# Fifteen seven-product pairs instead of fourteen in each half of the down projection

## The chip, the cores and the metric

The kernel runs on one core of a Trainium2 chip. The metric is the device time of one execution in microseconds (us). Five engines matter here: TensorE (PE: matmuls, with its weight loads PEld), VectorE (DVE), ScalarE (ACT), GpSimd (POOL) and SyncE (SP); the last two mostly issue DMAs in this kernel.

## The reference

One layer of an encoder on 256 positions of width 2048, all in float32: a mixer block (a gated MLP branch and a neighbourhood-attention branch, merged and projected), then a channel mixer, then a final RMSNorm. The change lies in the last matrix product of the channel mixer:

```python
def conv_ffn(x, g_norm, w_up, conv_k, conv_b, w_down):
    h = rms_norm(x, g_norm)
    up = h @ w_up                       # 256 x 2048 by 2048 x 11008
    ...                                 # centred depthwise convolution, width 3
    gate, val = jnp.split(up, 2, axis=-1)
    return x + (jax.nn.silu(gate) * val) @ w_down   # 256 x 5504 by 5504 x 2048
```

## The kernel before

**Precision.** TensorE has to give float32 products, so each operand is split into a high and a low part, and each product is three matmuls: high by high, low by high, high by low (`triple`). For a weight tile that comes from DRAM (`wraw`), ACT makes the high part (`whi`, line 172) and DVE the low part (`wlo`, line 173).

**The down projection.** It is worked off in two halves of 1024 output columns each (`g_dn[0]`, then `g_dn[1]`). The 5504 rows of the weights are 43 chunks of 128 rows: 21 pairs of chunks and a single one. A half therefore has 21 slots, 0 to 20, of two pieces each, and one last piece. A piece is 128 rows by 1024 columns of the weights, 512 KB, loaded by SP into one of five `wraw` buffers.

**Plain and seven-product slots.** A pair of chunks, two blocks of positions and two blocks of columns make a product of 2x2 by 2x2 blocks. A plain slot (P) does it in eight block products: 24 matmuls of 128x512. A seven-product slot does it in seven, by sums of blocks (Strassen's scheme in Winograd's form): 21 matmuls, 9 issued with the first piece (`r == 0`) and 12 with the second (`r == 1`). The sums of the activations are made in the up projection, one set for each pair in `DOWN_PAIRS` (`sums`, `sums_split`), written to DRAM, and read back by POOL's DMA queue (`stored`, line 1416). The sums of the weights come in one of two ways:

- Made slots (M): DVE makes four sums of 128x512 from the raw pieces (`weight_sums`, lines 362 to 366, into the tiles `t13` and `t24`), and ACT and DVE split them into `h13`, `l13`, `h24`, `l24` (`weight_sums_split`, lines 376 and 377), which the 12 matmuls of the second piece read. There is one tile of each name.
- Kept slots (K, the pairs in `DOWN_SPLIT`): the sums were made and split beside the up projection and written to DRAM; POOL's queue reads the four tiles of 512 KB back (`split_read`, line 1270), again into one tile of each name. SP loads only half of such a slot's first piece (256 KB).

**What sets the order.** The code is written out by hand: `begin(i)` issues the load of piece i + 5, the split of piece i + 3 and the tasks noted for piece i; then the matmuls of piece i are issued. A made slot that begins at piece i notes its sums at i - 3 and the split of its sums at i - 2 (`wide`). Reads of the kept sums are noted six pieces ahead, on one in-order queue with the reads of the activations' sums, which have three tiles in turn. Such a read can be issued once the matmuls that read the tile's former content are through. The last of them for `h24` and `l24` is the ninth matmul of a slot's second piece.

In the tiles' names of the profile and of the rows below, `h0` to `h5` are `t13`, `t24`, `h13`, `h24`, `l13`, `l24` of the made slots, and `h6`, `h7` and `s2` the three tiles for the activations' sums.

Of the kernel before, what the change touches and what calls it, by code (L numbers as in the profile page):

```python
# [67 lines left out]
TURN_X2 = (13, 1)  # L68
Y_GAP = 224
PAD = 16  # L70
DOWN_PAIRS = (2, 3, 5, 6, 7, 9, 10, 11, 13, 14, 15, 16, 17, 18)
DOWN_QUADS = ((1, 3, 5, 6, 7, 9, 10, 11, 13, 14, 15, 17, 18, 19), (1, 2, 4, 5, 6, 8, 9, 10, 12, 13, 14, 16, 17, 18))
DOWN_SPLIT = (2, 6, 10, 14, 17)
DOWN_JOBS = ((0, 2), (4, 6), (8, 10), (12, 14), (16, 18))
DOWN_LEADS = ({2: (4, 16, 16), 3: (5,), 5: (8,), 6: (7, 8, 8)}, {})
TWICE_AT = -15
# [4 lines left out]
def trunk_kernel(ctx, tc, x, x_t, vecs, w_in, ln_g, ln_b, w_st, b_s, rpb, w_branch, w_out, w_up, w_down,  # L81
# [26 lines left out]
    def bank():  # L108
        return psum.tile([128, 512], F32, name="bank")
# [76 lines left out]
            split_t[i] = (h, l)  # L186

    tasks = {}
    preload = {}

    def at(i, f):
        tasks.setdefault(i, []).append(f)
# [92 lines left out]

    def wide(src, row0, order, c0, acts, quads, room, done, sums=None, stored=None, split=None, late=False, lead=4, behind=(), ahead={}):
        n0 = plan_wide(src, row0, order, c0)
        boxes = {}
        for q in quads:
            i = n0 + 2 * q  # L290
            k = order[2 * q]
            units[i], units[i + 1] = 1, 2
            b = boxes[q] = {}
            ready = split[0].get(k // 2) if split else None
            if stored:
                b["acts"] = {}
                at(i - (ready[0] if ready else ahead.get(k // 2, lead)), lambda b=b, k=k: stored(k // 2, b["acts"]))
            else:
                b["acts"] = sums[k]
            if ready:  # L300
                halved.add(i)
                for n, lead in zip(("13", "24"), ready[-2:]):
                    at(i - lead, lambda b=b, k=k, n=n: split[1](k // 2, b, n))
                continue
            whole[i] = whole[i + 1] = None
            halves = late and q == quads[0]
            at(i - 3, lambda i=i, b=b, halves=halves: weight_sums(i, b, room, halves))
            if halves:
                at(i - 2, lambda b=b: b.pop("rest")())
            at(i - (1 if q in behind else 2), lambda b=b: weight_sums_split(b, room))  # L310
        return ("wide", n0, order, acts, quads, boxes, done)

# [59 lines left out]
    def weight_sums_split(box, room):  # L372
        u = []
        for name, t in zip(("13", "24"), box.pop("w")):
            h, l = room("h" + name, F32R), room("l" + name, F32R)
            nc.scalar.activation(h, t, AF.Copy)  # L376
            nc.vector.tensor_sub(l, t, h.bitcast(F32))
            u.append((h, l))
        split_sums(box, u)
# [5 lines left out]
    def run_wide(g, tail=0):  # L385
        kind, n0, order, acts, quads, boxes, done = g
# [19 lines left out]
        for i in range(n0, n1 - tail):  # L406
            begin(i)
            q, r = divmod(i - n0, 2)
            if C is None and q in quads:
                c = [bank() for _ in range(8)]  # L410
                P, C = [c[0], c[3], c[5], c[4]], [c[1:3], c[6:]]
            elif C is None:
                c = [bank() for _ in range(4)]
                C = [c[:2], c[2:]]
            if q not in quads:
                for t, c in ((0, 0), (0, 1), (1, 0), (1, 1)) if i > 1 else ((0, 0), (1, 0), (0, 1), (1, 1)):
                    plain(i, t, c)
                split_t.pop(i)
                continue
            st, sp = q == quads[0], q == quads[-1]  # L420
            k, k1 = order[2 * q:2 * q + 2]
            if r == 0:
                if P is None:
                    P = [bank() for _ in range(4)]
                (h0, l0), (h1, l1) = split_t[i], split_t[i + 1]
                triple(P[0], x_of(k, 0), h0[:, 0], l0[:, 0], st, sp)
                triple(C[0][0], x_of(k1, 0), h1[:, 0], l1[:, 0], first(0, 0), False)
                triple(C[0][1], boxes[q]["acts"]["s"][3], h1[:, 1], l1[:, 1], first(0, 1), False)
                split_t.pop(i)
                split_t.pop(i + 1)  # L430
                continue
            S, W = boxes[q]["acts"]["s"], boxes[q]["t"]
            triple(P[1], S[1], *W[1], st, sp)
            triple(P[3], S[0], *W[3], st, sp)
            triple(P[2], S[2], *W[2], st, sp)
            triple(C[1][0], x_of(k1, 1), *W[4], first(1, 0), False)
            if sp:
                done[0](P, i)
        if not tail:
            done[1](C, n1)  # L440
            return
# [803 lines left out]
    for n, (q, i, j) in enumerate(X_SUMS):  # L1245
        sum_acts_at(i, j, first_sums[2 * q], lambda q=q: q,
                    lambda name, dt, i=i: first_room("s2" if name == "f" and i < 16 else name, dt), f"s{n}", True)
# [97 lines left out]
    for n, (pair, g) in enumerate((pair, g) for g in range(2) for pair in OUT_SPLIT[g]):  # L1345
        t_kept[pair, g] = split_rows("out", pair, g)
        i = g_at[2 * n][1]
# [46 lines left out]
    for n, q in enumerate(OUT_PAIRS):  # L1394
        i = g_m2[0][1] + OUT_SUMS[n]
# [29 lines left out]
    def down_order(g):  # L1425
        free = [p for p in range(NF // 2) if p not in DOWN_PAIRS]
        kept = list(DOWN_PAIRS)
# [8 lines left out]
    for p, turn in zip(DOWN_SPLIT, DOWN_JOBS):  # L1436
        for g in range(2):
            d_kept[p, g] = split_rows("down", p, g)
            i = g_up[turn[g]][1]
# [180 lines left out]
```

## Time and profile before

| | |
|---|---|
| median of 3 runs | 1287.13 us (1286.27 to 1287.78) |
| profiled execution | 1286.73 us, of which the span of the instructions 1285.0 us |
| PE busy | 1275.3 us, 99% of the span, 6711 matmuls |
| DVE busy | 1128.1 us, 88% |
| ACT busy | 795.7 us, 62% |
| POOL busy | 173.6 us, 14% |
| DMA | 375.54 MB, mean 292 GB/s |
| granted TensorE clock | 0.999 of full speed |

The busy time of PE counts each matmul until its modelled end, and the ends of pipelined matmuls overlap; what a matmul costs a row of others is the distance from one start to the next. The up projection fills the span from about 604 to 1061 us, the first half of the down projection 1061 to 1169 us, the second 1169 to 1277 us.

### The profile page before, as it was taken

Reading aid. Unit: us, or ns where it says so; the run is one execution under the profiler, and the core shown is the slowest. Engines: PE = TensorE matmul, PEld = TensorE weight load, DVE = VectorE, ACT = ScalarE, POOL = GpSimd, SP = SyncE. Lnnn points to the kernel's source line nnn. Section 1 sums busy time; section 2 is a strip of 40 time slices with the busy share of each in tenths; the row PEclk is TensorE's granted clock in tenths of the full one; section 3 lists DMA queues with packets and bytes.
Section 4 is the critical chain, followed back from the end, with each engine's and each line's share of the span. In section 5 each row is a group of like instructions: output and inputs, shape, how many; then the busy total and the mean of one; then the engine's idle time right before and its main releaser. Section 6 shows DMA issues by size and latency. Waiting matters only on the chain.

```text
span 1285.0 us, 19793 instructions
## 1 busy us (share of the span) xinstructions
PE 1275.3 (99%) x6711; PEld 1088.0 (85%) x6711; DVE 1128.1 (88%) x1675; ACT 795.7 (62%) x1198; POOL 173.6 (14%) x328
## 2 busy tenths in 40 slices
PE   9999999999999999999999999999999999999997
PEld 7888888888888888888888888888888888888885
DVE  7898977777799988997989999899999989989988
ACT  7776575775755555565756666566566656555554
POOL 0003752330000001100000010011001001211210
PEclk9999999999999999999999999999999999999999
DMA  9789879989789977965877888888788779999993
GB/s 368 276 273 285 292 259 346 333 287 324 253 312 366 341 248 253 395 215 180 278 239 259 297 278 251 280 286 272 249 295 294 249 254 343 353 387 333 373 385 129
DMA packets 200485, 375.54 MB, mean 292 GB/s; under 512 B 16320, under 2 KB 124480, under 8 KB 200384
## 3 DMA queue, kind: packets, MB, share of 16 engines
q1 hardware_dynamic: 175472, 285.84, 64.3%
q0 software_dynamic: 24480, 87.78, 19.4%
q8 instruction: 52, 0.85, 0.3%
q10 hardware_dynamic: 432, 0.66, 0.1%
q14 instruction: 49, 0.40, 0.1%
HBM read 323.63 MB, written 48.50 MB: 290 GB/s over the span
## 4 chain that ended last, share of the span: by engine, by line
PE 98%; DVE 1%; issue 0%; ACT 0%; DVEq 0%; ACTq 0%
PE bank L224 31%; PE bank L228 16%; PE bank L321 12%; PE bank L319 11%; PE bank L320 11%; PE bank L252 5%; PE bank L254 5%; PE bank L253 5%; DVE wlo L173 1%; PE bank L873 0%; PE bank L827 0%; PE bank L500 0%; PE bank L862 0%; PE bank L700 0%; PE bank L1052 0%; PE bank L977 0%
## 5 line engine op out<-in xcount | busy, mean ns | idle before, releaser
L173 DVE TENSOR_TENSOR wlo<-wraw,whi 128x1024 fp32r<-128x1024 f32 (+1 forms) x472 | 535.7, 1149 | 113.3 <-ACT whi L172 72.1
L172 ACT ACTIVATE whi<-wraw 128x1024 fp32r<-128x1024 f32 (+1 forms) x472 | 461.1, 993 | 218.6 <-PE bank L320 54.6
L224 PE MATMUL bank<-h,whi 128*128 128x512 f32 x1760 | 423.4, 392 | 0.0
L224 PEld LDWEIGHTS bank<-h,whi 128*128 128x128 f32 x1760 | 323.0, 188 | 61.8
L228 PEld LDWEIGHTS bank<-h,wlo 128*128 128x128 f32 x1760 | 225.9, 191 | 8.8
L228 PE MATMUL bank<-h,wlo 128*128 128x256 f32 x1760 | 228.7, 283 | 0.0
L1084 ACT ACTIVATE tc<-ta,ck 128x256 f32<-128x256 f32 x86 | 47.1, 594 | 106.4 <-DVE ta L1082 106.4
L321 PE MATMUL bank<-wlo,a 128*128 128x512 f32 x204 | 79.8, 391 | 0.2 <-DVE wlo L173 0.2
L319 PE MATMUL bank<-whi,a 128*128 128x512 f32 x204 | 79.5, 390 | 0.0
L320 PE MATMUL bank<-whi,a 128*128 128x512 f32 x204 | 79.5, 389 | 0.0
L319 PE MATMUL bank<-whi,h 128*128 128x512 f32 x168 | 66.0, 393 | 0.0
L321 PE MATMUL bank<-wlo,h 128*128 128x512 f32 x168 | 65.6, 390 | 0.0
L320 PE MATMUL bank<-whi,h 128*128 128x512 f32 x168 | 65.4, 390 | 0.0
L1087 DVE SCALAR_TENSOR_TENSOR tc<-ta,ck,tc 128x255 f32<-128x255 f32 x86 | 41.4, 482 | 14.4 <-ACT tc L1084 14.4
L376 ACT ACTIVATE h<-h 128x1024 fp32r<-128x1024 f32 x36 | 38.0, 1058 | 21.1 <-DVE h L366 17.9
L1310 DVE TENSOR_TENSOR tw<-tw 128x512 f32<-128x512 f32 x72 | 50.2, 697 | 0.7
L252 PE MATMUL bank<-whi,h 128*128 128x512 f32 x128 | 50.4, 393 | 0.0
L252 PE MATMUL bank<-whi,y 128*128 128x512 f32 x128 | 50.3, 393 | 0.0
L253 PE MATMUL bank<-whi,y 128*128 128x512 f32 x128 | 49.9, 390 | 0.0
L253 PE MATMUL bank<-whi,h 128*128 128x512 f32 x128 | 49.9, 390 | 0.0
L254 PE MATMUL bank<-wlo,h 128*128 128x512 f32 x128 | 49.9, 390 | 0.0
L254 PE MATMUL bank<-wlo,y 128*128 128x512 f32 x128 | 49.9, 390 | 0.0
(327 smaller groups left out, 1981.2 us busy)
## 6 DMA issues: line engine op xcount, KB each, us to landing
wraw<-in_w_up_dram SPq DMA_DIRECT2D x336, 256.0 KB, 4.2
wraw<-in_w_in_dram SPq DMA_DIRECT2D x107, 512.0 KB, 6.3
wraw<-in_w_down_dram SPq DMA_DIRECT2D x76, 512.0 KB, 7.6
wraw<-in_w_in_dram SPq DMA_DIRECT2D x70, 256.0 KB, 4.3
wraw<-in_w_branch_dram SPq DMA_DIRECT2D x32, 512.0 KB, 5.5
wraw<-in_w_out_dram SPq DMA_DIRECT2D x28, 512.0 KB, 6.2
tw<-in_w_down_dram POOLq DMA_DIRECT2D x10, 1024.0 KB, 8.2
down_h<-so POOLq DMA_DIRECT2D x20, 512.0 KB, 3.7
```

The costliest lines, as they stand in the source:

```text
L172: nc.scalar.activation(h[:, k, :m], w[:, k, :m], AF.Copy)
L173: nc.vector.tensor_sub(l[:, k, :m], w[:, k, :m], h[:, k, :m].bitcast(F32))
L224: nc.tensor.matmul(p, h[:, k - k0, b * 128:(b + 1) * 128], acts(k), start=k == 0, stop=k == nk - 1)
L228: nc.tensor.matmul(p[:, :T], l[:, k - k0, b * 128:(b + 1) * 128], acts(k)[:, 0, :], start=False, stop=False)
L252: nc.tensor.matmul(p, xh, h[:, kk, :m], start=st, stop=False)
L253: nc.tensor.matmul(p, xl, h[:, kk, :m], start=False, stop=False)
L254: nc.tensor.matmul(p, xh, l[:, kk, :m], start=False, stop=sp)
L319: nc.tensor.matmul(p, xh, h, start=st, stop=False, **kw)
L320: nc.tensor.matmul(p, xl, h, start=False, stop=False, **kw)
L321: nc.tensor.matmul(p, xh, l, start=False, stop=sp, **kw)
L1084: nc.scalar.activation(v, u, AF.Identity, scale=ck[:, 1, ch:ch + 1], bias=ck[:, 3, ch:ch + 1])
L1310: nc.vector.tensor_add(w[:, d], w[:, a], w[:, b])
```

## The change

Pair 12, plain before, becomes a seven-product pair in both halves, made on the spot; and pair 11 changes places with pair 10 among the kept ones. The slots of the two halves, from 0 to 20 (P plain, M made, K kept):

```
half 0 before  P K P M P M K M P M K M P M K M P M K M P
half 0 after   P K P M P M K M P M M K M P M K M M K M P
half 1 before  P K M P M K M P M K M P M K M P M K M P P
half 1 after   P K M P M K M P M M K M P M K M M K M P P
```

In each half two made slots are neighbours at two places: slots 9 and 10, and 16 and 17, in half 0; 8 and 9, and 15 and 16, in half 1. There the split of the second slot's sums can't stand before the first slot's last matmuls, which read the same tiles; it is issued behind them (`after`). In the up projection pair 12 gets its activations' sums: four sums of 128x128 and two splits on DVE, two splits on ACT and one DMA on POOL.

```diff
-DOWN_PAIRS = (2, 3, 5, 6, 7, 9, 10, 11, 13, 14, 15, 16, 17, 18)
-DOWN_QUADS = ((1, 3, 5, 6, 7, 9, 10, 11, 13, 14, 15, 17, 18, 19), (1, 2, 4, 5, 6, 8, 9, 10, 12, 13, 14, 16, 17, 18))
-DOWN_SPLIT = (2, 6, 10, 14, 17)
+DOWN_PAIRS = (2, 3, 5, 6, 7, 9, 10, 11, 12, 13, 14, 15, 16, 17, 18)
+DOWN_QUADS = ((1, 3, 5, 6, 7, 9, 10, 11, 12, 14, 15, 16, 17, 18, 19), (1, 2, 4, 5, 6, 8, 9, 10, 11, 13, 14, 15, 16, 17, 18))
+DOWN_SPLIT = (2, 6, 11, 14, 17)
...
+    after = {}
...
-        boxes = {}
+        boxes, made = {}, set()
...
             whole[i] = whole[i + 1] = None
+            made.add(q)
             halves = late and q == quads[0]
             at(i - 3, lambda i=i, b=b, halves=halves: weight_sums(i, b, room, halves))
             if halves:
                 at(i - 2, lambda b=b: b.pop("rest")())
+            if q - 1 in made:
+                after[i - 1] = lambda b=b: weight_sums_split(b, room)
+                continue
             at(i - (1 if q in behind else 2), lambda b=b: weight_sums_split(b, room))
...
             if sp:
                 done[0](P, i)
+            if i in after:
+                after.pop(i)()
```

**DVE, half 1, slots 8 to 10.** Before, from the sums of slot 8 on (`h0`, `h1`), with slot 9 a kept one and slot 10 a made one:

```order
L363 TENSOR_TENSOR h1_12737<-wraw_12730,h1_12737 128x512
L173 TENSOR_TENSOR wlo_12757<-wraw_12730,whi_12756 128x1024
L377 TENSOR_TENSOR h4_12761<-h0_12736,h2_12760 128x1024
L377 TENSOR_TENSOR h5_12765<-h1_12737,h3_12764 128x1024
L173 TENSOR_TENSOR wlo_12785<-wraw_12754,whi_12784 128x512
L173 TENSOR_TENSOR wlo_12803<-wraw_12782,whi_12802 128x1024
L173 TENSOR_TENSOR wlo_12818<-wraw_12800,whi_12817 128x512
L365 TENSOR_TENSOR h0_12821<-wraw_12800 128x512
```

And now, from the same instruction on, with slot 9 a made one and slot 10 a kept one:

```order
L368 TENSOR_TENSOR h1_12754<-wraw_12747,h1_12754 128x512
L173 TENSOR_TENSOR wlo_12774<-wraw_12747,whi_12773 128x1024
L382 TENSOR_TENSOR h4_12778<-h0_12753,h2_12777 128x1024
L382 TENSOR_TENSOR h5_12782<-h1_12754,h3_12781 128x1024
L173 TENSOR_TENSOR wlo_12810<-wraw_12771,whi_12809 128x512
L370 TENSOR_TENSOR h0_12813<-wraw_12771 128x512
L371 TENSOR_TENSOR h0_12813<-wraw_12771,wraw_12807 128x512
L367 TENSOR_TENSOR h1_12814<-h0_12813,wraw_12807 128x512
L368 TENSOR_TENSOR h1_12814<-wraw_12807,h1_12814 128x512
L173 TENSOR_TENSOR wlo_12834<-wraw_12807,whi_12833 128x1024
L173 TENSOR_TENSOR wlo_12851<-wraw_12831,whi_12850 128x512
L382 TENSOR_TENSOR h4_12867<-h0_12813,h2_12866 128x1024
```

Four sums stand now between the two pieces of slot 9, and the two splits of its sums (the last row and the one that follows it) stand behind the low part of the first piece of slot 10.

**SP, half 0, from the loads of slot 6's second piece on.** A row of 128x512 is the half piece of a kept slot; the rows between count the other pieces. Before:

```order
L147 DMA wraw<-in_w_down_dram 128x1024 x7
L147 DMA wraw<-in_w_down_dram 128x512
L147 DMA wraw<-in_w_down_dram 128x1024 x7
L147 DMA wraw<-in_w_down_dram 128x512
L147 DMA wraw<-in_w_down_dram 128x1024 x7
L147 DMA wraw<-in_w_down_dram 128x512
L147 DMA wraw<-in_w_down_dram 128x1024 x8
```

And now:

```order
L147 DMA wraw<-in_w_down_dram 128x1024 x9
L147 DMA wraw<-in_w_down_dram 128x512
L147 DMA wraw<-in_w_down_dram 128x1024 x7
L147 DMA wraw<-in_w_down_dram 128x512
L147 DMA wraw<-in_w_down_dram 128x1024 x5
L147 DMA wraw<-in_w_down_dram 128x512
L147 DMA wraw<-in_w_down_dram 128x1024 x8
```

The kept slots were four slots apart (a half piece and seven pieces); now they are five, four and three apart. POOL's queue of reads keeps its order: the reads of pair 17's kept sums (slot 18) still come behind those of pair 14's (slot 14 before, slot 15 now), into the same tiles. In half 1 the last two kept slots are likewise three apart (14 and 17, before 13 and 17).

## Rows read from the trace of the kernel before

**Rows 1.** The page's busy line (section 1) and its chain by engine (section 4).

```profile
PE 1275.3 (99%) x6711; PEld 1088.0 (85%) x6711; DVE 1128.1 (88%) x1675; ACT 795.7 (62%) x1198; POOL 173.6 (14%) x328
...
PE 98%; DVE 1%; issue 0%; ACT 0%; DVEq 0%; ACTq 0%
```

**Rows 2.** Windows: busy us of PE, PEld, DVE, ACT, POOL; clock, DMA share, GB/s.

```profile
670.90:693.20 22.30, 22.30 (x130) 19.72 (x129) 20.89 (x41) 13.96 (x25) 1.26 (x2) 1.00 0.90 309
893.60:915.90 22.30, 22.30 (x130) 19.72 (x129) 19.90 (x36) 13.31 (x23) 0.71 (x1) 1.00 0.87 299
1061.10:1168.80 107.70, 107.70 (x475) 88.80 (x474) 98.30 (x124) 61.68 (x74) 19.70 (x38) 1.00 0.97 363
```

**Rows 3.** Waits of PEld, down projection: total us, times, longest.

```profile
PEld bank L321 <- DVE wlo L173: 1.1, 3, 0.6
```

**Rows 4.** Timeline of PE, down projection: start us, modelled length, instruction.

```profile
1108.99 0.39 PE L319 MATMUL bank<-h,h 128*128 128x512 f32 x1
...
1136.19 0.39 PE L319 MATMUL bank<-whi,a 128*128 128x512 f32 x1
...
1213.71 0.39 PE L319 MATMUL bank<-whi,a 128*128 128x512 f32 x1
...
1223.23 0.39 PE L319 MATMUL bank<-whi,a 128*128 128x512 f32 x1
...
1228.67 0.39 PE L319 MATMUL bank<-whi,a 128*128 128x512 f32 x1
...
1238.19 0.39 PE L319 MATMUL bank<-whi,a 128*128 128x512 f32 x1
```

**Rows 5.** Timeline of POOL, half 0, the reads for slot 18.

```profile
1135.97 0.54 POOL L1416 DMA_DIRECT2D s<-sums  x1 [4.21 <-PE bank L321]
...
1138.07 0.53 POOL L1270 DMA_DIRECT2D l<-down_l  x1
```

**Rows 6.** Tile down_l, two reads, 1137.03 and 1138.07 us.

```profile
DMA to landing us min/median/max: 8.0/10.2/12.4
```

**Rows 7.** Tile down_l, the reads for half 1's slot 17 (1238 to 1243 us).

```profile
L1270 POOL DMA_DIRECT2D l<-down_l x2: 528/532/537, 1239.2 to 1240.2; - x2
...
DMA to landing us min/median/max: 5.8/7.9/10.1
```

**Rows 8.** Tile down_l, 1096 to 1245 us: 16 reads for eight kept slots.

```profile
DMA to landing us min/median/max: 5.8/10.2/13.5
```

**Rows 9.** Timeline of DVE, half 1, slot 8's sums and splits; start us, length.

```profile
1203.87 0.69 DVE L365 TENSOR_TENSOR h<-wraw 128x512 f32<-128x512 f32 x1
1204.47 0.69 DVE L366 TENSOR_TENSOR h<-wraw 128x512 f32<-128x512 f32 x1
1205.08 0.69 DVE L362 TENSOR_TENSOR h<-h,wraw 128x512 f32<-128x512 f32 x1
1205.80 0.69 DVE L363 TENSOR_TENSOR h<-wraw,h 128x512 f32<-128x512 f32 x1
1206.41 1.22 DVE L173 TENSOR_TENSOR wlo<-wraw,whi 128x1024 fp32r<-128x1024 f32 x1
1207.55 2.36 DVE L377 TENSOR_TENSOR h<-h,h 128x1024 fp32r<-128x1024 f32 x2
1209.82 0.69 DVE L173 TENSOR_TENSOR wlo<-wraw,whi 128x512 fp32r<-128x512 f32 x1
```

**Rows 10.** Timeline of ACT, half 1, the pieces after slot 8.

```profile
1210.37 1.06 ACT L172 ACTIVATE whi<-wraw 128x1024 fp32r<-128x1024 f32 x1 [2.18 <-DMA wraw<-in_w_down_dram]
1212.91 0.63 ACT L172 ACTIVATE whi<-wraw 128x512 fp32r<-128x512 f32 x1 [1.48 <-DMA wraw<-in_w_down_dram]
```

**Rows 11.** Timeline of DVE, half 0, the splits of slot 9's sums.

```profile
1104.36 2.36 DVE L377 TENSOR_TENSOR h<-h,h 128x1024 fp32r<-128x1024 f32 x2
```

**Rows 12.** Timeline of ACT, half 0, the pieces after slot 9.

```profile
1108.24 1.06 ACT L172 ACTIVATE whi<-wraw 128x1024 fp32r<-128x1024 f32 x1 [3.24 <-DMA wraw<-in_w_down_dram]
1110.85 0.63 ACT L172 ACTIVATE whi<-wraw 128x512 fp32r<-128x512 f32 x1 [1.55 <-DMA wraw<-in_w_down_dram]
```

## The prediction

> **What bounds the kernel now.** I read the page first, and there the busy line and the chain that ended last: 98% of the chain is TensorE [rows 1]. Then the timeline of PE in the down projection, where the change is. From the first matmul of a plain slot to the first of the next slot, 24 matmuls, it takes 1228.67 - 1223.23 = 5.44 us, 0.227 us each [rows 4]: this is the price of a 128x512 matmul in a row of others. Last the waits. Of the weight loads that feed PE, those on DVE's low parts come to 1.1 us in all, in three places [rows 3]. PE is the bound and hardly waits, so a matmul taken away is time taken away, as long as what feeds PE stays ahead. Little stays ahead by much: in the first half DVE is busy 98.30 of 107.70 us and the DMA engines 0.97 of the time [rows 2].
>
> **What is removed.** In each half one plain slot of 24 matmuls becomes one of 21. Six matmuls at 0.227 us are **-1.36 us**. All stand on the chain.
>
> **The up projection.** Pair 12 now makes its activations' sums one block of the up projection after its own, beside the second part of a kept pair's preparation. The stretch in which this falls (893.6 to 915.9 us) has DVE busy for 19.90 of 22.30 us; a stretch of the same kind that already has such sums, pair 2's (670.9 to 693.2 us), has 20.89, and PE fills both [rows 2]. So DVE takes 1.0 us more in a stretch with 2.4 us left, PE's matmuls cover it, and it costs **0**. Were that cover gone it would cost at most the 1.0 us.
>
> **The kept slots that came closer.** This is the term I think decides the sign. POOL's reads for a kept slot can only be issued when the kept slot before it is through with the tiles. Before, in half 0, slot 14 ended at 1136.19 [rows 4]. The five reads for slot 18 were issued from 1135.97 to 1138.07 [rows 5]; the last of them, `l24`, landed 12.4 us after its issue [rows 6], at 1150.5, so 14.3 us after the end of slot 14. The matmul that first reads `l24` is the ninth of the kept slot's second piece. With three slots between them there were 21 + 24 + 21 + 9 + 8 matmuls until then, 18.8 us: 4.5 us to spare. Now slot 15 is followed by two made slots, and `l24` is wanted after 21 + 21 + 9 + 8 = 59 matmuls, 13.4 us. A landing at 14.3 us is 0.9 us late, and PE stands for that long, with nothing to do meanwhile: **+0.9 us**. In half 1 the nearest row is the read for slot 17: slot 13 ended at 1238.19 [rows 4], the second `l` read was issued at 1240.2 and landed after 10.1 us [rows 7], 12.1 us after the end of slot 13. By that row it is 1.3 us early: **0**. Over all the eight kept slots' reads the landing took at most 13.5 us [rows 8], which with the issue 1.9 us after the slot's end makes 15.4 us, 2.0 us late; so each place has bounds of 0 and 2.0 us. A gain is excluded, since nothing waited there before. The other kept slots keep four slots' distance or gain one. The activations' sums for slot 19 come behind these reads in POOL's queue, but are wanted a whole slot (4.8 us) later.
>
> The Trainium skill ("DMA: Bandwidth & Descriptors", section "Anatomy of one DMA — SWDGE (gpsimd) path") gives such a DMA some 2.0 us and its bytes at 436 GB/s; for the four tiles of 512 KB and the 384 KB of sums together that is an estimate of 7.7 us from the first issue, and nothing would be late. The trace doesn't agree: one read alone takes up to 13.5 us to land [rows 8]. The reads there share the engines with SP's loads, and the sum would be -1.36 us by the rule and -0.5 us by the rows.
>
> **The neighbours.** A made slot costs DVE four sums at 0.60, 0.61, 0.72 and 0.61 us, the low parts at 0.60 and 1.14 us, and two splits at 1.14 us (distances of starts, [rows 9]): 6.6 us, where PE needs 21 x 0.227 = 4.8 us. Two of them in a row lose 3.6 us of DVE's lead. I walked the place where DVE's lead is smallest by my reading, slots 8 and 9 of half 1. DVE is through with slot 8's splits at 1209.82 [rows 9]. Then stand the low part of slot 9's first piece (to 1210.42), and the sums: the first to 1211.03, the second wants the second piece, landed by 1210.37 [rows 10], so all four are done at 1212.97, and that piece's low part at 1214.1 (0.08 us later to be read, since an instruction's length is 1.22 and its distance 1.14). PE's slot 9 starts at 1213.71 [rows 4], and its sixth matmul reads it at 1214.85: 0.7 us in hand. Next the first piece of slot 10, landed at 1212.91 [rows 10], low part at 1214.7. Now the moved split. ACT can make `h13` as soon as the sixth matmul of slot 8's second piece is through, near 1212.4, and behind the high part of slot 10's first piece, so 1213.5 to 1214.6; DVE makes `l13` from 1214.7 to 1215.9. PE wants it 9 + 2 matmuls after 1213.71, at 1216.2: **0.3 us in hand**. `l24` is ready at 1217.1 and wanted at 1217.6. So the moved split just passes. In half 0, DVE is through with slot 9's splits at 1106.63 [rows 11], 2.4 us before PE wants them at 1108.99 [rows 4], but the next slot's second piece lands only at 1108.24 [rows 12]. The same steps from there put the four sums at 1110.2, that piece's low part at 1111.3, the high part of the following half piece (landed 1110.85, [rows 12]) at 1111.5 and its low part at 1112.1, `h13` at 1112.5, `l13` at 1113.6, and PE wants it at 1114.2: 0.6 us in hand. The other two places come after a kept and a made slot behind a plain one, where DVE has had more time. I take **0** for all four. The bound on the other side: landing times of loads move by up to 2 us or so (as the reads' do in rows 6 to 8), which beyond 0.3 and 0.6 us in hand would cost 1.7 and 1.4 us at the first two places. What queues behind the moved split is the next low part on DVE and the next high part on ACT; PE wants these a slot later.
>
> **Sum.** -1.36 + 0 + 0.9 + 0 = -0.5 us. The profiled execution took 1286.73 us, 1.7 us of it around the span of 1285.0; the change moves only the span, so 1286.2 us. The median of the runs lies 0.4 us above the profiled one, at 1287.13, which gives **1286.6 us**.
>
> **The rivals.** Faster or slower by over 0.2% means 2.6 us, which is about what a measurement of this kernel can tell from no change.
>
> - *The reads land in time.* If they land within 13.4 us of the former kept slot's end in half 0 as well, no wait takes the place of the matmuls: 1287.13 - 1.36 = 1285.8 us. It speaks for it that one of the two cases worked out above lands at 12.1 us; against it, that the other, 14.3 us, is the one of this half. Chance 0.33. By the Trainium skill's figures above it would come so.
> - *DVE comes late at the neighbours.* It speaks for it that 0.3 us is little and that two neighbours overdraw DVE by 3.6 us; against it, that the walks above use the landings of that very stretch, in which the bytes asked for hardly change. With loads 1 us later it costs 0.7 + 0.4 us: 1287.7 us. With 2 us it costs 3.1: 1289.7 us, slower. Chance 0.15, a third of it slower.
> - *The kept reads are late at both places* (the other side). Late by 2.0 us at each is the bound by rows 8: 1287.13 - 1.36 + 4.0 = 1289.8 us, slower by 0.2%. It decides from landings of 15.4 us after the former kept slot's end on, at both. It speaks for it that three made or kept slots in a row ask for more bytes in less time than with a plain one between, with DMA engines 0.97 busy; against it, 12.1 us in half 1. Chance 0.08.
> - *More is won than the matmuls.* Were PE's waits of 1.1 us on low parts gone too, it would be 1284.7 us, still within 0.2%; they lie before the changed slots, though, so I leave 0.04 for anything that makes it faster by over 0.2%.
>
> **How the numbers follow.** The forecast itself (one place late by some 0.9 us) has 0.40. With the reads in time (0.33) and the milder part of a late DVE (0.10) there is 0.83 for no change that can be told; slower 0.08 + 0.05 = 0.13; faster 0.04. The range runs from 1285.2, half a microsecond below the second case for the scatter of the runs (1286.27 to 1287.78), to 1289.2, where two places are late by 1.7 us each.
>
> **What would show it.** In the profile after: 6705 matmuls, still 0.227 us apart. A wait of PE or PEld on `l<-down_l` in half 0 at slot 18, of some 0.9 us, near 1154 us, and none or less at slot 17 of half 1. The last `l` read landing some 14 us after slot 15's end. At the moved splits, ACT's `h13` waiting for PE, and no wait of PE on `h4` or `h5`. I am wrong if PE waits there for DVE, or if the waits on the kept reads reach 2 us each.

## The result and the profile after

The changed kernel takes 1289.18 us (median of 22 runs, 1287.84 to 1291.68), the kernel before, on the same chips, 1287.01 us (22 runs): the ratio is 1.0017 with a 95% interval of 1.0011 to 1.0023. It is slower by some 2.2 us, where 0.5 us faster was forecast. That is inside the stated range (1285.2 to 1289.2 us), at its end, and on the other side of no change. It is less than the 0.2% that the prediction took for what can be told from no change; 22 runs of each can tell it.

The page of the changed kernel, its busy line and its chain, which answer to [rows 1]:

```profile
PE 1275.7 (99%) x6705; PEld 1086.1 (84%) x6705; DVE 1137.1 (88%) x1693; ACT 800.1 (62%) x1204; POOL 175.4 (14%) x331
...
PE 93%; DVE 3%; DMA 1%; issue 1%; ACT 1%; DVEq 0%; ACTq 0%; SPq 0%
```

Six matmuls are gone, and TensorE's share of the chain fell from 98% to 93%: the chain now runs through DVE, ACT and DMAs, so PE waits. Its waits in the down projection (total us, times, longest), where the kernel before had 1.1 us of PEld in all [rows 3]:

```profile
PE bank L326 <- DVE wlo L173: 1.9, 2, 1.1
PE bank L326 <- DMA l<-down_l: 0.2, 1, 0.2
...
PEld bank L326 <- DVE wlo L173: 3.5, 5, 1.5
PEld bank L326 <- DMA l<-down_l: 0.9, 2, 0.6
PEld bank L326 <- DVE h L382: 0.5, 1, 0.5
```

A wait stands under PEld and under PE, so the lines can't be added up. To place them, I took the distances between the starts of neighbouring matmuls and summed what goes beyond 0.227 us. Before, that is 0.71 us in the whole down projection (0.24 in slots 0 and 1, 0.47 in the last four pieces). After, it is 3.65 us: 0.27 in slots 0 and 1, 0.45 at half 0 slot 18, **1.11 at half 1 slot 4**, 0.36 at half 1 slot 16, 0.11 at slot 17 and 1.36 in the last four pieces. Three of these on PE's timeline (start, modelled length, instruction; in brackets idle time and what ended it):

```profile
1154.76 0.39 PE L325 MATMUL bank<-h,h 128*128 128x512 f32 x1
1155.33 0.50 PE L326 MATMUL bank<-l,h 128*128 128x512 f32 x1 [0.18 <-DMA l<-down_l]
...
1190.61 0.39 PE L325 MATMUL bank<-whi,a 128*128 128x512 f32 x1
1191.84 0.50 PE L326 MATMUL bank<-wlo,a 128*128 128x512 f32 x1 [0.83 <-DVE wlo L173]
...
1251.63 0.40 PE L325 MATMUL bank<-h,s 128*128 128x512 f32 x1
1252.10 0.50 PE L326 MATMUL bank<-h,s 128*128 128x512 f32 x1
```

The first is the kept read `l24` at slot 18, the second the low part of the second piece of half 1's slot 4, the third `l13` of a moved split. The second is the large one, and the prediction has nothing at that place: slots 0 to 6 of half 1 are the same as before.

The sum of the two profiled executions: 2.94 us more waits, 0.57 us by which the whole down projection starts later (1061.06 and 1061.63 us; the difference is there in the first microseconds of the kernel, and the other kernels below lie from 1061.05 to 1062.29, e11_late and e16_bevac, whose up projection is that of before, at 1061.43 and 1061.42, so it is scatter), less 1.36 us of matmuls: 2.15 of the 2.4 us between the spans (1285.0 and 1287.4).

**Where the 1.11 us come from.** At the border of the halves DVE takes half 0's product sums out of PSUM: five instructions on the banks (lines 1005 to 1009 here, 998 to 1002 before), then the rest of it. In its order of instructions they stand behind the low part of half 1's first piece. DVE's timeline there, before:

```profile
1159.63 2.36 DVE L173 TENSOR_TENSOR wlo<-wraw,whi 128x1024 fp32r<-128x1024 f32 x2
1161.90 0.69 DVE L998 TENSOR_TENSOR x<-bank,x 128x512 f32<-128x512 f32 x1
```

and after:

```profile
1160.47 1.22 DVE L173 TENSOR_TENSOR wlo<-wraw,whi 128x1024 fp32r<-128x1024 f32 x1 [0.81 <-ACT whi L172]
1163.42 1.23 DVE L173 TENSOR_TENSOR wlo<-wraw,whi 128x1024 fp32r<-128x1024 f32 x1 [1.73 <-ACT whi L172]
1164.57 0.68 DVE L1005 TENSOR_TENSOR x<-bank,x 128x512 f32<-128x512 f32 x1
```

Before, the two low parts run back to back. After, DVE stands idle for 1.73 us ahead of that low part; the row names ACT, but ACT waited for the load:

```profile
1162.33 1.06 ACT L172 ACTIVATE whi<-wraw 128x1024 fp32r<-128x1024 f32 x1 [1.89 <-DMA wraw<-in_w_down_dram]
```

The load of that piece, before (issue of the DMA, and the time to its landing):

```profile
L147 SPq DMA_DIRECT2D wraw<-in_w_down_dram x1: 328/328/328, 1152.8 to 1152.8; - x1
...
DMA to landing us min/median/max: 6.7/6.7/6.7
```

and after:

```profile
L147 SPq DMA_DIRECT2D wraw<-in_w_down_dram x1: 327/327/327, 1152.7 to 1152.7; - x1
...
DMA to landing us min/median/max: 9.5/9.5/9.5
```

Issued at the same time, it lands 2.8 us later. What is new in those microseconds is on POOL's queue:

```profile
1142.04 0.53 POOL L1277 DMA_DIRECT2D h<-down_h  x1 [0.16 <-issue]
...
1143.61 0.53 POOL L1277 DMA_DIRECT2D l<-down_l  x1
...
1146.63 1.07 POOL L1581 DMA_DIRECT2D gfin<-in_norm_final_dram  x2
1151.17 0.54 POOL L1423 DMA_DIRECT2D s<-sums  x1 [3.46 <-PE bank L325]
1154.78 0.53 POOL L1277 DMA_DIRECT2D h<-down_h  x1 [3.07 <-PE bank L326]
```

The reads for slot 18 that began at 1135.97 us before [rows 5] begin at 1141.34 now, and behind them come two reads of the final norm's weights (`gfin`, 256 KB each). Before, the queue's reads up to `gfin` had landed by 1154.69 us; now by 1159.57, so they share the DMA engines with that load for most of its way. What each queue moved between that load's issue and its landing (q0 is POOL's queue, q1 SP's; packets, MB, share of the engines' time), before:

```profile
q1 hardware_dynamic: 433, 1.57, 59.4%
q0 software_dynamic: 202, 0.85, 35.5%
```

and after:

```profile
q0 software_dynamic: 519, 2.06, 53.4%
q1 hardware_dynamic: 522, 1.88, 49.0%
```

Of the 1.5 MB more, 1.2 are POOL's and 0.3 are of SP's own earlier loads. The Trainium skill has the rule ("DMA: Bandwidth & Descriptors", section "Queues, rings and completion order"): each DMA engine takes turns between the queues that have work for it. The trace agrees: SP's load asks for the same bytes, and takes 9.5 us where POOL's queue moves 2.06 MB beside it and 6.7 us where it moves 0.85.

### The profile page after: what moved, and what is told of

Read it like the earlier page. It is cut to its first block, busy times and chain, and to the rows that moved or that the text cites. A ratio compares the mean times of both kernels' runs of the same rounds, so it can differ in the third digit from the quotient of the medians.

```text
span 1287.4 us, 19813 instructions
## 1 busy us (share of the span) xinstructions
PE 1275.7 (99%) x6705; PEld 1086.1 (84%) x6705; DVE 1137.1 (88%) x1693; ACT 800.1 (62%) x1204; POOL 175.4 (14%) x331
## 4 chain that ended last, share of the span: by engine, by line
PE 93%; DVE 3%; DMA 1%; issue 1%; ACT 1%; DVEq 0%; ACTq 0%; SPq 0%
PE bank L225 31%; PE bank L229 16%; PE bank L326 10%; PE bank L324 10%; PE bank L325 10%; PE bank L253 5%; PE bank L255 5%; PE bank L254 5%; DMA wraw<-in_w_down_dram 1%; DVE wlo L173 1%; ACT whi L172 0%; PE bank L880 0%; PE bank L834 0%; PE bank L507 0%; PE bank L869 0%
## 5 line engine op out<-in xcount | busy, mean ns | idle before, releaser
L326 PE MATMUL bank<-wlo,a 128*128 128x512 f32 x194 | 76.0, 392 | 1.9 <-DVE wlo L173 1.9
L325 PE MATMUL bank<-whi,a 128*128 128x512 f32 x194 | 75.5, 389 | 0.0
L324 PE MATMUL bank<-whi,a 128*128 128x512 f32 x194 | 75.5, 389 | 0.0
L381 ACT ACTIVATE h<-h 128x1024 fp32r<-128x1024 f32 x40 | 42.4, 1060 | 21.4 <-DVE h L371 10.7
```

What stands on the lines that cost most here:

```text
L324: nc.tensor.matmul(p, xh, h, start=st, stop=False, **kw)
L325: nc.tensor.matmul(p, xl, h, start=False, stop=False, **kw)
L326: nc.tensor.matmul(p, xh, l, start=False, stop=sp, **kw)
```

## The experiments

Two theories stood against each other from the second group on. *Reads*: the loss comes from the last reads of half 0 being 5 us later, at the kept slot and at the border. *DVE*: the fifteenth seven-product slot asks more of DVE than it has. Medians are of 11 runs (e8_pool: 5), ratios against the kernel before on the same chip. "Wait" is the sum of distances beyond 0.227 us in the one profile of each kernel. The profiled run needn't be like the median: its time is the lowest of the eleven in e7_l24 (1287.26 us) and the highest in e4_light (1289.26 us), so a profile shows where a run waits, and the size of a gain is read from the medians.

**e1_half0.** The new slots in half 0 alone; in the half where pair 12 is plain, this kernel and the next read a block of activations that holds pair 12's fourth sum, so that part of the result is another. The lines that give each half its own lists are left out here.

```diff
-DOWN_QUADS = ((1, 3, 5, 6, 7, 9, 10, 11, 12, 14, 15, 16, 17, 18, 19), (1, 2, 4, 5, 6, 8, 9, 10, 11, 13, 14, 15, 16, 17, 18))
+DOWN_QUADS = ((1, 3, 5, 6, 7, 9, 10, 11, 12, 14, 15, 16, 17, 18, 19), (1, 2, 4, 5, 6, 8, 9, 10, 12, 13, 14, 16, 17, 18))
...
```

> Half 0 has the new slots, half 1 the old ones (pair 12 plain there, pair 10 kept); the up projection is the changed kernel's. Three matmuls fewer than before, -0.7 us. DVE theory (the 4 us of DVE work that the made slot adds in half 0 is missing as lead where DVE has most to do, at half 1's slots 2 to 4 and at the end): the wait of 1.0 us at half 1's slot 4 stays, the end's wait returns to its 0.5 us; some 1287.0 + 0.5 (kept read at slot 18) + 1.0 - 0.7 = 1287.8 us. Kept-read theory (only the reads in POOL's queue are late, the rest is scatter): 1287.0 + 0.5 - 0.7 = 1286.8 us.

1289.06 us, ratio 1.0015 (1.0006 to 1.0024). Waits: 0.45 us at half 0 slot 3, 0.66 at slot 18, 1.42 at half 1 slot 4. The loss belongs to half 0's change, slot 4 of the unchanged half 1 with it.

**e2_half1.** The new slots in half 1 alone.

```diff
+DOWN_QUADS = ((1, 3, 5, 6, 7, 9, 10, 11, 13, 14, 15, 17, 18, 19), (1, 2, 4, 5, 6, 8, 9, 10, 11, 13, 14, 15, 16, 17, 18))
...
```

> Half 1 has the new slots, half 0 the old ones. Three matmuls fewer, -0.7 us. DVE theory: half 0 hands over the same lead as before, so there is no wait at half 1's slot 4; the waits at slots 16 and 17 and the longer wait at the end (0.9 us more) stay: 1287.0 - 0.7 + 0.5 + 0.9 = 1287.7 us. Kept-read theory: 1287.0 - 0.7 + 0.1 = 1286.4 us, and the end's wait as before.

1287.13 us, ratio 1.0001 (0.9992 to 1.0010). No wait at slot 4; 0.64 us for the kept read at slot 17, about what its three matmuls (0.68 us) win.

**e3_cols.** The products with the final norm's weights, which DVE makes in slots 3 and 4 of half 1 (1185.0 to 1190.6 us), moved 20 pieces later.

```diff
-            at(i + 4 + j, lambda j=j: columns(j))
+            at(i + 24 + j, lambda j=j: columns(j))
```

> The changed kernel, with the four products by the final norm's weights (DVE, 2.4 us) moved from pieces 4 and 5 of half 1 to pieces 24 and 25. DVE theory: DVE gets 2.4 us more lead at half 1's slot 4, so the wait of 1.1 us there goes; some 0.3 us of it may come back at slot 16: 1289.2 - 1.0 = 1288.2 us. Load theory (DVE is late at slot 4 because the loads land late): DVE waits for the loads instead, and it stays at 1289.2 us.

1289.38 us, ratio 1.0018 (1.0009 to 1.0027). The wait at slot 4 is gone; 1.17 + 0.36 us stand at slot 16 instead, and 1.14 for the kept read at slot 17. So work on DVE is part of the chain to slot 4, and at the one other place tried it costs as much.

**e4_light.** Pair 12's four weight sums and their splits left out in both halves; it multiplies by its own plain blocks (another result), with the same matmuls and reads.

```diff
+            if stored and k // 2 == 12:
+                units[i] = 2
+                b["plain"] = True
+                continue
...
```

> The changed kernel, with pair 12's sums of weights left out: its four products of the second piece read that piece's own split blocks, so DVE does for pair 12 what it does for a plain pair, in both halves; matmuls, activations' sums, reads and the places of the kept slots are the changed kernel's. DVE theory: DVE's work is that of the kernel before, the waits at half 1's slot 4 and at the end fall back to those of before: 1287.0 - 1.4 + 0.6 (kept reads) = 1286.2 us. If the new spacing of the kept slots or the moved splits are what costs: near 1289.2 us.

1287.86 us, ratio 1.0007 (0.9998 to 1.0015). 1.3 us better than the change by the medians (the ratio's interval still overlaps the change's a little), so DVE's added work is likely to have a part in the loss. Its profile, of the run with the highest time, still has 1.79 us at half 1 slot 4 and 0.40 and 0.75 at the two kept reads: these waits come without DVE's added work too. Where the 1.3 us were won, that profile can't show.

**e5_k19.** Half 0 with fourteen pairs, its last kept slot at 19 and the one before at 15; half 1 as before.

```diff
+DOWN_QUADS = ((1, 3, 5, 6, 7, 9, 10, 11, 12, 14, 15, 16, 18, 19), (1, 2, 4, 5, 6, 8, 9, 10, 12, 13, 14, 16, 17, 18))
+DOWN_SPLIT = ((2, 6, 11, 15, 18), (2, 6, 10, 14, 17))
...
```

> Half 0 has before's fourteen pairs, but its last kept slot stands four slots after the one at 15 (at 19) instead of four after 14 (at 18), and half 0 has one pair of neighbours (slots 9 and 10, split as in the changed kernel); half 1 is before's, so 6711 matmuls as before. So POOL reads for the last kept slot start some 5 us later than before and run over into half 1, while no slot is added. Theory reads (POOL's reads that back up across the border of the halves make SP's first loads of half 1 land later, which takes DVE's lead at half 1 slot 4): no wait at the kept slot, loads of half 1's first pieces land 1 to 2 us later after their issue than before, PE waits 0.5 to 1.5 us at half 1 slot 4, total 1287.6 to 1288.6 us. Theory DVE (the added made slot's sums take the lead): no slot is added, slot 4 waits nothing, 1287.0 us.

1287.06 us, ratio 1.0003 (0.9994 to 1.0012). The reads are 5 us later as in the change, and nothing waits for them. The first load of half 1 took 8.5 us, and DVE, which had stood idle for 1.70 us ahead of the piece before it, stood idle for 0.04 ahead of this one; the five instructions still began early enough for slot 4 (table below). While that load was on its way POOL's queue moved 0.91 MB and SP's 2.46, so here SP's own loads have the larger part in its delay. The expectation of the reads theory failed: a later read by itself cost nothing here; it has to meet a shorter distance.

**e6_gfin.** The two `gfin` reads 16 pieces earlier on POOL's queue.

```diff
-FIN_AT = 36
+FIN_AT = 20
```

> The changed kernel, with the two 256 KB reads for the final columns issued on POOL 16 pieces earlier in half 0, so they are not in the queue with the kept reads of its last kept slot. Theory reads: the queue is 0.5 MB shorter at the border of the halves, the wait at half 1 slot 4 (1.1 us in the changed kernel) falls to 0 to 0.5 us, 1288.3 us. Theory DVE: the wait stays at 1.1 us, 1289.2 us.

1288.20 us, ratio 1.0011 (1.0003 to 1.0020). Half 1's first load took 8.5 us instead of 9.5, and slot 4 waits 0.18 us, as the reads theory had it. But the same profile has 0.51 and 1.41 us at the two kept reads, and 3.6 us of waits in all, as much as the change's. The gain of 1.0 us by the medians is not clear of the scatter (the ratio's interval overlaps the change's, 1.0011 to 1.0023), and that it comes by this load isn't shown, since the two later kernels with this edit had 9.1 and 10.4 us in their profiles.

**e7_l24.** A second tile for `l24`, read alone eight pieces ahead.

```diff
...
+                if ahead:
+                    at(i - max(ready[-1], L24_AHEAD), lambda b=b, k=k: split[1](k // 2, b, "l24"))
...
+        if name == "l24":
+            ff["l24"] = ff.get("l24", 1) ^ 1
+            if ff["l24"]:
+                return ff["third"].tile([128, 2, 512], F32R, name="l24b")
...
```

> The changed kernel, with a second tile for the read l24, which is issued alone eight pieces ahead of a kept slot; the four other reads stay where they are. The step of the prediction (l24 is the late read, 0.45 us in half 0 slot 18 of the changed kernel and 0.1 in half 1 slot 17): both waits go, -0.6 us. Theory reads: the queue's backlog at the border is 0.25 MB shorter, and the wait at half 1 slot 4 falls by some 0.3 to 0.6 us as well: 1288.0 to 1288.6 us. Theory DVE: slot 4 as in the changed kernel, or 0.45 us later since PE no longer gives DVE that time back before: 1289.2 us.

1288.74 us, ratio 1.0015 (1.0006 to 1.0024). The waits on the reads are gone from the profile, half 1's first load still took 9.7 us and slot 4 waits 1.27. The median is 0.4 us below the change's, which is within the scatter; the hoped-for relief at slot 4 did not come.

**e8_pool.** DVE's four multiplications by the final norm's weights given to POOL.

```diff
-        nc.vector.tensor_mul(c, c, fin["g", j])
+        nc.gpsimd.tensor_mul(c, c, fin["g", j])
```

> The changed kernel, with the four multiplications of the final columns (0.6 us each on DVE) done by POOL. They stand on DVE between half 1's pieces 4 and 10. If DVE's own work there is what PE waits for at half 1 slot 4, 2.4 us less of it takes that wait (1.1 us) away, whatever took the lead before: 1288.1 us. If only the landing of the loads held DVE, the wait stays: 1289.2 us. POOL may hold DVE's next step (the columns' first addition) if its multiplication is long.

1291.99 us, ratio 1.0039 (1.0026 to 1.0053): worse by 2.8 us than the change, with 2.61 + 1.06 us at slot 4. POOL's row and two of DVE's beside it (rows of DVE from its own timeline):

```profile
1182.89 7.49 POOL L1143 TENSOR_TENSOR x<-x,gfin 128x512 f32<-128x512 f32 x4
```

```profile
1187.46 1.78 DVE L370 TENSOR_TENSOR h<-wraw 128x512 f32<-128x512 f32 x1
1189.16 1.77 DVE L371 TENSOR_TENSOR h<-wraw 128x512 f32<-128x512 f32 x1
1190.85 0.68 DVE L367 TENSOR_TENSOR h<-h,wraw 128x512 f32<-128x512 f32 x1
```

Four such products take POOL 7.49 us there, and DVE's own sums take 1.78 us while they run and 0.68 once they are through. The run says nothing on the theories: what it took off DVE it gave back by slowing the rest.

**e9_both.** e6_gfin and e7_l24 together (their two edits).

> The changed kernel with both of the last two edits: the reads for the final columns 16 pieces earlier and l24 read alone into a second tile. Theory reads (what the changed kernel loses lies in its reads: late ones at the kept slots, and two sets of them 13 us apart instead of 19 at the border of the halves, which make SP's loads late and so DVE at half 1 slot 4): the two edits take away different waits, so 1289.2 - 1.0 - 0.45 = 1287.7 us. Theory DVE (fifteen pairs ask more of DVE than it has, and whatever is taken away at one place comes back at the next): no better than the better edit alone, 1288.2 us or more.

1287.35 us, ratio 1.0002 (0.9993 to 1.0011). The median is 1.8 us below the change's, no less than the two edits' gains together (1.0 and 0.4 us), against the DVE theory. Its profile still has 1.31 us at slot 4, with a load of 9.1 us.

**e11_late.** The kernel before; the activations' sums for slot 19 are read ahead of slot 18's, so that slot 18's reads stand behind a read that waits for slot 15.

```diff
-DOWN_LEADS = ({2: (4, 16, 16), 3: (5,), 5: (8,), 6: (7, 8, 8)}, {})
+DOWN_LEADS = ({2: (4, 16, 16), 3: (5,), 5: (8,), 6: (7, 8, 8), 17: (6, 1, 1), 18: (9,)}, {})
```

> The kernel before, 6711 matmuls, with one thing changed: the five reads for half 0's slot 18 stand on POOL's queue behind a read that waits for slot 15, so they start some 5 us later (near 1141.5 us instead of 1136), 13 us ahead of the reads for half 1's slot 1 as in the changed kernel. DVE's work is before's. Theory reads: l24 lands within half a microsecond of when slot 18 wants it (wait 0 to 0.5 us), the first loads of half 1 land 1.5 to 3 us later after their issue than before, and PE waits 0.5 to 1.2 us at half 1 slot 4, where before had 0.58 us in hand: 1287.6 to 1288.7 us. Theory DVE: no wait at slot 4, 1287.0 to 1287.3 us.

1290.06 us, ratio 1.0021 (1.0012 to 1.0030): with no work added on any engine, the later reads alone cost 2.8 us. In the profile they cost it at the kept slot:

```profile
1155.73 0.40 PE L320 MATMUL bank<-h,h 128*128 128x512 f32 x1
1157.89 0.50 PE L321 MATMUL bank<-l,h 128*128 128x512 f32 x1 [1.77 <-DMA l<-down_l]
```

`l24`, issued at 1143.50 us, landed after 14.35 us. The whole wait at the slot is 2.33 us; it gives DVE that time, and slot 4, though half 1's first load took 9.2 us, waits for nothing. The right sign, but at the kept slot, where the reads theory had 0 to 0.5 us, and not at slot 4. What the run does show is the load: with SP's pieces those of before, it lands after 9.2 us when POOL's queue is late, and what the queues moved while it was on its way is as in the change:

```profile
q0 software_dynamic: 526, 1.95, 52.3%
q1 hardware_dynamic: 522, 1.88, 50.2%
```

**e12_noread.** The change without the four reads for half 1's slot 1, which multiplies by the blocks that slot 18 left (another result).

```diff
+            if (pair, g) == (2, 1) and queue is nc.gpsimd:
+                u.append(kept["last"][n])
+                if len(u) == 2:
+                    split_sums(box, u)
+                return
...
```

> The changed kernel without the four reads (2 MB) for half 1's slot 1, which multiplies by the blocks that half 0's slot 18 left in the tiles (that part of the result is another). Theory reads: the first loads of half 1 land as early as before, and the wait at half 1 slot 4 (1.1 us) is gone or below 0.3 us: 1288.0 us, about as much as from moving the final columns' reads. Theory DVE: the wait at slot 4 stays, 1289.2 us.

1290.01 us, ratio 1.0021 (1.0012 to 1.0030): a miss. Half 1's first load took 9.5 us as in the change, the two after it 8.3 and 5.7 us instead of 10.6 and 9.0. DVE there:

```profile
1164.69 1.23 DVE L173 TENSOR_TENSOR wlo<-wraw,whi 128x1024 fp32r<-128x1024 f32 x1 [1.58 <-ACT whi L172]
1165.83 0.69 DVE L1005 TENSOR_TENSOR x<-bank,x 128x512 f32<-128x512 f32 x1
```

and slot 4 waits 1.64 us. So the reads for slot 1 are not the cause, and the later loads are not either: the first load is what is left. Why this kernel is 0.8 us slower than the change (its profile has 1.23 us at half 0 slot 17 and 1.55 at half 1 slot 17) stays open.

**e13_h1l24.** e2_half1 with e7_l24's edit.

> Half 1 changed, half 0 as before (1287.13 us when run so), with l24 read alone and early into a second tile. The wait of that kernel on l24 at half 1 slot 17 was 0.64 us; by both theories it goes and nothing takes its place, 1286.5 us. As there, in the half where pair 12 is plain it reads a block that holds pair 12's fourth sum.

1286.32 us, ratio 0.9995 (0.9987 to 1.0004). The wait on `l24` is gone; 0.33 + 0.36 us at half 1 slot 16 are in its profile (of a run of 1287.28 us, 1.0 above the median), so something of it can come back on DVE.

**What the profiles have in common.** Half 1's first load, the start of the first of the five instructions counted from half 1's first matmul, and the wait at half 1 slot 4, worked out from the profile of each:

```
              load us   start us   wait us
e2_half1        5.7      -7.37      0
before          6.7      -6.93      0
e5_k19          8.5      -6.33      0
e6_gfin         8.5      -5.67      0.18
change          9.5      -4.74      1.12
e1_half0        9.9      -4.42      1.43
e12_noread      9.5      -4.20      1.64
e4_light       10.2      -4.05      1.80
```

Where there is a wait it is the start plus 5.85 us, to 0.01: what stands between the two on DVE and ACT passes the delay on whole. The waits of e7_l24 and e9_both (1.27 and 1.31 us) follow it too; e3_cols and e8_pool, which change DVE's work between the two, don't. And the load sets the start: from its landing to the start of the first of the five instructions it is 2.34 us in every kernel in which that load is late and the five stand behind that piece's low part. This made the third group.

**e14_evac.** The change with the five DVE instructions (and one on ACT) recorded at once, ahead of the split of half 1's first piece.

```diff
-            at(i + 1, first_half)
+            if j == 0 and room is down_room:
+                first_half()
+            else:
+                at(i + 1, first_half)
```

> The changed kernel; on DVE and ACT the first six instructions that take half 0's product sums out of PSUM (one on ACT, five on DVE) stand ahead of the split of half 1's first piece instead of behind it. In the profiles so far with half 0 changed, DVE stands idle for 1.2 to 1.7 us for that piece's load with these five behind it, and the wait at half 1 slot 4 is the start of the first of them, counted from half 1's first matmul, plus 5.85 us. Theory reads, in this form (late reads delay that load; the order on DVE passes the delay on): DVE is through with this work 0.9 to 1.6 us earlier, the wait of 1.1 us falls to 0 to 0.3 us, and 1289.2 becomes 1288.1 to 1288.4 us, with the wait on l24 left. Theory DVE (there is too much work on DVE, in whatever order): the wait moves, 1289.2 us.

1288.38 us, ratio 1.0012 (1.0003 to 1.0022). DVE's timeline:

```profile
1161.15 1.23 DVE L173 TENSOR_TENSOR wlo<-wraw,whi 128x1024 fp32r<-128x1024 f32 x1 [1.18 <-ACT whi L172]
1162.30 0.68 DVE L1005 TENSOR_TENSOR x<-bank,x 128x512 f32<-128x512 f32 x1
...
1164.93 0.69 DVE L1009 TENSOR_TENSOR h<-bank,h 128x512 f32<-128x512 f32 x1
1165.54 2.35 DVE L173 TENSOR_TENSOR wlo<-wraw,whi 128x1024 fp32r<-128x1024 f32 x2
```

The load took 9.5 us again, but the five instructions run while it is on its way, the low parts follow without a gap, and slot 4 waits for nothing. That the wait there comes by this order is shown; the 0.8 us by which the median is lower are not clear of the scatter by themselves (the ratio's interval overlaps the change's). The waits on `l24` (0.46 us in each half), 0.38 us at half 0 slot 17 and 1.2 in the last four pieces are left.

**e15_three.** e9_both and e14_evac together (their three edits).

> The changed kernel with three edits together: the final columns' reads earlier, l24 alone and early into a second tile (1287.35 us with these two), and the product sums of half 0 taken out ahead of the split of half 1's first piece. Theory reads: the 1.3 us at half 1 slot 4 that the profile of the two edits still had go to 0 to 0.3 us, 1286.2 to 1286.6 us, the six matmuls' worth below before. Theory DVE: 1287.3 us.

1286.47 us, ratio 0.9998 (0.9989 to 1.0007). The one line of PEld's waits in its down projection:

```profile
PEld bank L329 <- DVE wlo L174: 2.0, 4, 1.0
```

No kept read and no moved split is waited for; slot 4 has 0.29 us left (with a load of 10.4 us), the last four pieces 0.87. By its median this is the fastest kernel here with the whole result, 2.7 us below the change, but it can't be told from the kernel before.

**e16_bevac.** The control: the kernel before with e14_evac's edit.

> Control: the kernel before with the product sums of half 0 taken out ahead of the split of half 1's first piece. There the load has landed when DVE comes to it and slot 4 has 0.58 us in hand, so both theories expect no change: 1287.0 us. If it is faster by itself, the last two runs say nothing of the change.

1286.82 us, ratio 0.9999 (0.9990 to 1.0008). Without the late load the order costs nothing, so what e14_evac and e15_three win is the change's own loss, and e15_three's 2.7 us are well clear of the scatter.

## Why the prediction was wrong

- *The matmuls.* 6705, still 0.227 us apart: -1.36 us, right.
- *The up projection.* The window of pair 12's block, and the down projection's first half, which answer to [rows 2]:

```profile
894.00:916.30 22.30, 22.30 (x130) 19.71 (x129) 20.89 (x41) 13.89 (x24) 1.25 (x2) 1.00 0.91 310
1061.63:1169.29 107.66, 107.48 (x472) 88.17 (x471) 100.16 (x126) 63.56 (x76) 20.29 (x39) 1.00 0.96 360
```

  DVE has 20.89 us of 22.30 where 20.9 was worked out, PE has no gap: 0, right.
- *The kept read in half 0.* `l24` landed 11.7 us after its issue, which answers to the 12.4 us of [rows 6], and 13.7 us after the end of slot 15, where 14.3 was forecast:

```profile
L1277 POOL DMA_DIRECT2D l<-down_l x2: 528/531/534, 1142.6 to 1143.6; - x2
...
DMA to landing us min/median/max: 7.9/9.8/11.7
```

  The wait is 0.45 us for 0.9, and 0.40 to 0.88 in the other profiles with the change's slots in half 0 and `l24` unmoved, but for e12_noread, where PE came late itself. Place and mechanism are right, the size forecast is double what was measured. In half 1, 0 was forecast; the change's profile has 0.11, others with its half 1 have 0.30 to 1.55 us, so 0 was too kind.
- *The neighbours.* 0 in all four places was forecast. Three have none. By the timelines `l13` is ready 0.65 us before use at half 1 slot 9 (forecast 0.3), and 0.92 at half 0 slot 10 (forecast 0.6). At half 1 slot 16, which I had passed over as having "had more time", PE waits 0.36 us. Half 0 slot 17, passed over with it, has no wait in the change's profile, but waits 0.25 to 0.39 us for `l13` in those of e3_cols, e8_pool, e12_noread and e14_evac. So the two places that were walked held, and the two that were not are the ones that wait.
- *The step that failed* is the one that I thought decides the sign, "the kept slots that came closer". It priced the later reads at the matmul that reads them and nowhere else, and it saw what stands behind them in POOL's queue as harmless. They also take DMA time from SP's load of half 1's first piece (9.5 for 6.7 us), which DVE's order puts ahead of the sums' way out of PSUM, and so 1.11 us arrive at half 1 slot 4, 28 us later. I asked who waits for POOL's queue, and not who shares the DMA engines with it, though [rows 2] showed them 0.97 busy and I used that row for a rival. No rival names this path; "DVE comes late" has the right engine and the right cause (loads later), at another place. The runs show it from three sides: that load takes 8.5 to 10.4 us in all thirteen kernels in which half 0's last kept reads are late, and 5.6 to 6.9 us in the four in which they are not; in e11_late the late reads alone, with SP's loads and DVE's work those of before, make it 9.2 us (the 2.8 us of that run were lost at the kept slot, and don't count for this path); and the wait at slot 4 goes when the order on DVE is turned, though the load stays late. Late reads are not the only thing that can delay the load (e5_k19), and the 1.1 us are only a part of the loss: 0.56 us are the kept reads', 0.36 a neighbour's, and DVE's added work is likely to have a part (e4_light) that these profiles don't place; that stays open.
- *What the last four pieces cost* (0.47 us before, 1.36 after) I don't put down to the change: it is 1.51 us in e5_k19 and 1.15 in e11_late, whose half 1 is that of before, and 0.06 in e12_noread. What sets it was not tried.

With the three edits together (e15_three) the time came to 0.5 us below before, the value forecast, but that is luck: the term of 0.9 is gone there, and waits for DVE in half 1 have its place.

## What to carry to other kernels

When a transfer moves in time, list who shares the DMA engines with it at its new place, not only who waits for it; then follow each late load through the in-order engine that meets it, down to what is queued behind. Where an engine takes finished sums out of PSUM, see whether that work stands behind the first operand of the next stage; here that operand's load took between 5.6 and 10.4 us, and the work could go ahead of it at no cost (e16_bevac). And walk every place that a change makes tighter, not only the ones that look tightest: a gain of 1.36 us is soon lost when four or five places can each take some tenths of a microsecond to one.

## What the runs showed of the hardware

POOL's product of two 128x512 float32 tiles from SBUF takes 1.87 us (7.49 for four, beside DVE's work) where DVE's takes 0.68, and DVE's own sums of the same form take 1.78 instead of 0.68 us beside it. The Trainium skill ("GPSIMD Engine Reference", section "1. Specifications") says that POOL shares its way to SBUF with DVE and contends with DVE instructions that have two SBUF inputs; these rows agree, and put the price at 2.6 times on DVE's side.

The same load of 512 KB, issued at the same point of the kernel, takes between 5.6 and 10.4 us in these kernels: 5.6 to 6.9 us where POOL's queue moved 0.41 to 0.85 MB beside it, and 9.2 to 10.2 us in the eight kernels where it moved 1.95 to 2.14 MB. Meanwhile the two queues together moved 363 to 420 GB/s in every profile, so the time goes with the sum of their bytes. A kept read of 512 KB took up to 14.8 us in the change and up to 15.6 in e5_k19.
